# Loading a matrix product's 32-row block tiles in eight pieces on one issuing engine instead of four pieces on two

## The chip, the cores and the metric

One core of a Trainium2 chip. The metric is the device time of one execution in microseconds, median over the runs of a kernel. Each kernel also has one profiled run; its span (first to last instruction) is some 2 us shorter than its time. In names of engines: PE is the matmul engine, DVE, ACT and POOL are the vector, scalar and general engines, SP only issues DMAs; "ACTq" and "SPq" are ACT's and SP's instruction queues. A run is called slow when it is over 1.5% above the fastest of the same kernel.

## The reference

```python
# x: 16 x 512 x 768, weight: 768 x 768, cos and sin: 512 x 64, all float32; 12 heads of 64
y = np.matmul(x, weight).reshape(16, 512, 12, 64)
y1, y2 = y[..., :32], y[..., 32:]
out1 = y1 * cos1 - y2 * sin1
out2 = y2 * cos2 + y1 * sin2
out = np.concatenate([out1, out2], axis=-1).reshape(16, 512, 768)
```

## The kernel before

The input is cut into 64 tiles of 128 rows, worked through as 32 pairs. A tile is loaded (384 KB), cast to fp16 by ACT, turned (rows to columns), multiplied by the weight on PE (12 matmuls), multiplied by cos and sin on DVE, added up on POOL, and stored, one 768 KB store per pair, three pairs later.

There are two ways to turn a tile. A plain tile is turned by six PE transposes and copied back from the accumulator memory by ACT (`xT`). A **block tile**, the second tile of some odd pairs, is loaded so that each 32x32 block lies where DVE can turn it in one instruction, which saves PE 0.34 us. That load is made of four pieces, one per quarter of the partitions.

```python
    def load(n, s):                       # a plain tile, on SP
        ...
        nc.sync.dma_start(out=xss[n, s], in_=...)

    def load_blocks(n):                   # a block tile
        ...
        src = x[b].rearrange("(j a r) (q k) -> r q a j k", r=SB, a=R, q=NQ)
        dst = xss[n, 1].rearrange("p (j k) -> p j k", j=NQ)
        for q in (0, 2, 1, 3):
            eng = nc.sync if q < 2 else nc.scalar
            eng.dma_start(out=dst[ts(q, R)], in_=src[r, q])
    ...
    for n in range(2, NP):
        load_plain(n + AHEAD - 2)
        if n + 1 < NP and by_blocks(n + 1, 1):
            transpose_blocks(n + 1, 1)
        for s in (0, 1):
            for c in CHUNKS:
                mm(n, s, *c)
            upto("turn", 2 * n + s + 3)   # PE transposes, ACT copy to xT
            upto("cast", 2 * n + s + 5)   # ACT
            ...
        if n >= 3:
            store(n - 3, nc.scalar)       # issued by ACT
        load_blocks(n + AHEAD_B)
        if n < NP - ALONE:
            rope_pair(n, 2 * H if n < NP - ALONE - 1 else H)
```

`nc.sync` is SP, `nc.scalar` is ACT, `nc.gpsimd` is POOL. Every engine works through its instructions in order, so an engine that issues DMAs and also computes can be held up by an issue.

## Time and profile before

| | before |
|---|---|
| time, median of 4 runs of the comparison | 164.53 us (164.27 to 165.13) |
| span of the profiled run, granted clock | 162.5 us, 0.988 |
| PE busy | 150.2 us, 92% |
| holes of PE after 17 us, start to start | 2.64 us |
| ACT, DVE, POOL busy | 91.2, 120.8, 110.2 us |
| DMAs per two pairs | 3 plain loads, 4 pieces, 2 stores: 9 |

A hole is the time from the start of one group of matmuls to the start of the next, less what the group takes undisturbed (1.95 us for the 12 matmuls of a tile, 0.34 us for six transposes). Two pairs take PE 4 x 1.95 + 3 x 0.34 = 8.82 us if it never waits. The rows of the page that count the DMA issues will matter (bytes each, then median us from issue to landing):

```profile
out_dram<-ov ACTq DMA_DIRECT2D x31, 768.0 KB, 6.5
xs<-in_x_dram SPq DMA_DIRECT2D x53, 384.0 KB, 6.4
...
xb<-in_x_dram SPq DMA_DIRECT2D x22, 96.0 KB, 6.4
xb<-in_x_dram ACTq DMA_DIRECT2D x22, 96.0 KB, 6.3
```

A piece of 96 KB takes as long from issue to landing as a store eight times its size.

### The profile page before, as it was taken

What the parts mean: (1) busy time and instruction counts of PE and PEld (TensorE: products, weight loads), DVE (VectorE), ACT (ScalarE), POOL (GpSimd) and SP (SyncE); (2) the same over time, 40 slices, a digit from 0 to 9 for tenths busy, and PEclk for the clock granted to TensorE, in tenths of its full rate; (3) what the DMA queues carried; (4) which work ended last, traced back from release to release, by engine and by line L of the source; (5) the groups of instructions that cost most, each with busy time, mean ns of one, the idle gap of its engine ahead of it and who ended that gap; (6) DMA issues with size and microseconds to landing.
All of it is one profiled execution on the core that took longest, in us unless ns stands there. A gap on an engine that the chain in (4) does not pass through costs nothing.

```text
span 162.5 us, 2775 instructions
## 1 busy us (share of the span) xinstructions
PE 150.2 (92%) x1104; PEld 94.4 (58%) x1104; DVE 120.8 (74%) x68; ACT 91.2 (56%) x114; POOL 110.2 (68%) x40
## 2 busy tenths in 40 slices
PE   7799999999998999999999999999989899999910
PEld 2355666666564656666666666666656466666600
DVE  0666976788878587988878787879787756889970
ACT  3431866764665556764765756867293998610000
POOL 0000397777887767778888787877868774699990
PEclk9999999999999999999999999999999999999995
DMA  4999999999999999999999999999997545459766
GB/s 156 358 412 396 403 396 314 384 361 299 381 369 324 399 310 406 316 401 328 405 316 397 350 384 370 371 375 344 320 373 231 196 194 198 194 208 391 283 244 232
DMA packets 24141, 53.17 MB, mean 327 GB/s; under 512 B 2368, under 2 KB 8384, under 8 KB 24128
## 3 DMA queue, kind: packets, MB, share of 16 engines
q1 hardware_dynamic: 12096, 25.89, 47.9%
q10 hardware_dynamic: 12032, 27.10, 43.6%
q8 instruction: 8, 0.13, 0.3%
q14 instruction: 5, 0.04, 0.1%
HBM read 27.82 MB, written 25.17 MB: 326 GB/s over the span
## 4 chain that ended last, share of the span: by engine, by line
PE 51%; DMA 27%; DVE 7%; ACT 6%; issue 2%; ACTq 2%; SPq 1%; POOLq 1%; POOL 1%; DVEq 0%
PE psy L169 43%; DMA xs<-in_x_dram 13%; DMA xb<-in_x_dram 10%; PE pt L126 7%; DVE tq L183 7%; DMA w_raw<-in_weight_dram 4%; ACT xc L76 4%; ACT xT L76 2%; ACTq L243 1%; SPq L83 1%; POOLq L363 1%; POOL ov L194 1%; ACTq L102 0%; ACTq L76 0%; POOLq L194 0%
## 5 line engine op out<-in xcount | busy, mean ns | idle before, releaser
L194 POOL TENSOR_TENSOR ov<-tq 128x1536 f32<-128x1536 f32 (+2 forms) x36 | 110.0, 3067 | 47.9 <-DVE tq L183 47.1
L169 PE MATMUL psy<-w_sb,xT 128*128 128x512 f16 (+1 forms) x744 | 129.7, 326 | 0.8 <-ACT xT L76 0.8
L183 DVE TENSOR_TENSOR tq<-psy,csn 128x3072 f32<-128x3072 f32 (+3 forms) x37 | 103.4, 2807 | 28.7 <-PE psy L169 28.7
L169 PEld LDWEIGHTS <-xT 128*128 128x128 f16 x768 | 72.9, 98 | 45.6 <-ACT xT L76 1.9
L76 ACT COPY xT<-pt 128x768 f16<-128x768 f16 x51 | 40.5, 800 | 36.7 <-PE pt L126 29.2
L76 ACT CAST xc<-xs 128x768 f16<-128x768 f32 x51 | 44.8, 904 | 9.1 <-DMA xs<-in_x_dram 8.1
L126 PE MATMUL pt<-ident,xc 128*128 128x128 f16 x318 | 26.0, 219 | 2.6 <-ACT xc L76 1.6
L126 PEld LDWEIGHTS <-xc 128*128 128x128 f16 x318 | 21.6, 98 | 11.0 <-ACT xc L76 3.6
L76 ACT CAST xc<-xb 128x768 f16<-128x768 f32 x11 | 10.0, 905 | 5.8 <-DMA xb<-in_x_dram 5.8
L247 PE MATMUL cold_ps<-cold 128*128 128x512 f16 x16 | 6.0, 521 | 1.2 <-DVE cold L252 1.2
L133 DVE STREAM_TRANSPOSE xT<-xc 128x384 f32<-128x384 f32 x11 | 6.2, 568 | 0.0
L110 DVE CAST w_sb<-w_raw 128x768 f16<-128x768 f32 x6 | 3.3, 558 | 2.0 <-DMA w_raw<-in_weight_dram 2.0
L78 DVE CAST xc<-xs 128x768 f16<-128x768 f32 x2 | 1.9, 954 | 3.7 <-DMA xs<-in_x_dram 3.7
L169 PE MATMUL psz<-w_sb,xT 128*128 128x512 f16 (+1 forms) x24 | 4.2, 326 | 0.0
L247 PEld LDWEIGHTS <-cold 128*128 128x128 f16 x16 | 1.8, 126 | 3.4 <-issue 2.2
L183 DVE TENSOR_TENSOR tq<-psz,csn 128x1024 f32<-128x1024 f32 (+1 forms) x4 | 3.6, 945 | 0.0
L78 DVE COPY xT<-pt 128x768 f16<-128x768 f16 x2 | 1.1, 556 | 1.3 <-PE pt L126 1.3
L76 ACT ACT_TABLE_LOAD x1 | 1.3, 1283 | 1.1 <-PEq L349 1.1
L252 DVE MEMSET cold<- 128x256 uint32 x1 | 0.3, 272 | 0.9 <-PEq L349 0.9
L148 PE MATMUL psy<-cold 128*128 128x512 f16 x2 | 0.8, 379 | 0.0
L226 DVE TENSOR_TENSOR ov<-psy,tq 128x512 f32<-128x512 f32 x1 | 0.7, 691 | 0.0
L222 DVE TENSOR_TENSOR psy<-psy,csn 128x512 f32<-128x512 f32 x1 | 0.7, 690 | 0.0
(8 smaller groups left out, 1.7 us busy)
## 6 DMA issues: line engine op xcount, KB each, us to landing
out_dram<-ov ACTq DMA_DIRECT2D x31, 768.0 KB, 6.5
xs<-in_x_dram SPq DMA_DIRECT2D x53, 384.0 KB, 6.4
w_raw<-in_weight_dram SPq DMA_DIRECT2D x6, 384.0 KB, 7.6
xb<-in_x_dram SPq DMA_DIRECT2D x22, 96.0 KB, 6.4
xb<-in_x_dram ACTq DMA_DIRECT2D x22, 96.0 KB, 6.3
out_dram<-ov ACTq DMA_DIRECT2D x1, 384.0 KB, 3.4
out_dram<-ov SPq DMA_DIRECT2D x1, 256.0 KB, 2.4
csn<-in_cos_dram SPq DMA_DIRECT2D x1, 128.0 KB, 7.2
```

The source lines that it names most:

```text
L76: eng.copy(out=o, in_=i_)
L78: eng.tensor_copy(out=o, in_=i_)
L83: nc.sync.dma_start(out=xss[n, s], in_=x[b].rearrange("(p r) h -> r p h", r=SB)[r])
L110: nc.vector.tensor_copy(out=w_sb[:, t, e], in_=w_raw[:, t, e])
L126: nc.tensor.transpose(pt[:, t, e, :], xc[:, t, e, :], ident)
L133: nc.vector.transpose(out=xT.bitcast(FP32).rearrange("p t m e -> p (t m e)"), in_=x16.pop((n, s)).bitcast(FP32),)
L169: nc.tensor.matmul(ps, xTT[n, s][:, t, e, :], w_sb[:, t, e, lo:hi], start=((t, e) == CHUNKS[0] and not joined), stop=((t, e) == CHUNKS[-1] ...
L183: nc.vector.tensor_tensor(out=tqs[n][:, :, c0:c1].rearrange("p j (h d) -> p j h d", d=D), in0=ps.rearrange("p (h d) -> p h d", d=D) .unsqu ...
L194: eng.tensor_tensor(out=ovs[n][:, ds(c0, w)].rearrange("p (h t d) -> p h t d", t=2, d=HD), in0=tq[:, 0].rearrange("p (h t d) -> p h t d", ...
L243: eng.dma_start(out=dst, in_=src)
L247: nc.tensor.matmul(cold_ps, cold[:, 0:P], cold, start=True, stop=True)
L363: with _tile.TileContext(nc) as tc:
```

## The change

The intent: free ACT from issuing pieces, keep both halves of the partitions busy by taking lower and upper quarters in turn, issue the pieces earlier, and shorten the end by treating the last eight tiles singly.

```diff
-    AHEAD_B = 4
-    ALONE = 3
+    AHEAD_B = 6
+    ALONE = 4
...
-        return s == 1 and n % 2 == 1 and 6 < n < NP - ALONE
+        return s == 1 and n % 2 == 1 and 8 < n < NP - ALONE
...
-    bpool = ctx.enter_context(tc.tile_pool(name="bpool", bufs=AHEAD_B + 1))
+    bpool = ctx.enter_context(tc.tile_pool(name="bpool", bufs=3))
-    tpool = ctx.enter_context(tc.tile_pool(name="tpool", bufs=9))
+    tpool = ctx.enter_context(tc.tile_pool(name="tpool", bufs=11))
...
-        for q in (0, 2, 1, 3):
-            eng = nc.sync if q < 2 else nc.scalar
-            eng.dma_start(out=dst[ts(q, R)], in_=src[r, q])
+        for q in (0, 1):
+            for j in range(0, NQ, 2):
+                for h in (q, q + 2):
+                    nc.sync.dma_start(
+                        out=dst[ts(h, R), j : j + 2], in_=src[r, h, :, j : j + 2]
+                    )
...
-        k += min(4, max(0, k - 41) // 4)
+        k += min(6, max(0, k - 31) // 4)
...
+                    store(n, nc.scalar, s * H, (s + 1) * H)
-        if n >= 3:
-            store(n - 3, nc.scalar)
         load_blocks(n + AHEAD_B)
         if n < NP - ALONE:
-            rope_pair(n, 2 * H if n < NP - ALONE - 1 else H)
-    store(NP - 3, nc.scalar)
-    store(NP - 2, nc.scalar)
-    store(NP - 1, nc.scalar, 0, H)
+            if n >= 3:
+                store(n - 3, nc.scalar)
+            rope_pair(n, H if n == NP - ALONE - 1 else 2 * H)
+        if n == NP - ALONE - 1:
+            for m in (n - 2, n - 1, n):
+                store(m, nc.scalar)
```

## The prediction

> **What bounds the kernel now.** I read the page's slices first, then the timeline of the matmul engine, then the timeline of ACT where the matmul engine stood still, then the waits of the SP queue, and last the end of the run.
>
> The slices (tenths busy of forty 4.06 us slices, then GB/s):
>
> ```profile
> PE   7799999999998999999999999999989899999910
> DMA  4999999999999999999999999999997545459766
> GB/s 156 358 412 396 403 396 314 384 361 299 381 369 324 399 310 406 316 401 328 405 316 397 350 384 370 371 375 344 320 373 231 196 194 198 194 208 391 283 244 232
> ```
>
> PE is busy nearly throughout, and so is the DMA until the last input lands at about 125 us. Once stores have begun, good slices reach 400 GB/s and every second one sinks to 300-330.
>
> The timeline of PE: one tile is 12 matmuls that start 1.95 us apart from tile to tile, and six PE transposes add 0.34 us. Only four times after the start does the next group come late:
>
> ```profile
> 48.64 2.11 PE L169 MATMUL psy<-w_sb,xT 128*128 128x256 f16 x12
> 51.37 2.12 PE L169 MATMUL psy<-w_sb,xT 128*128 128x512 f16 x12 [0.61 <-ACT xT L76]
> ...
> 60.50 2.12 PE L169 MATMUL psy<-w_sb,xT 128*128 128x512 f16 x12 [0.16 <-ACT xT L76]
> ...
> 120.82 0.51 PE L126 MATMUL pt<-ident,xc 128*128 128x128 f16 x6 [0.46 <-ACT xc L76]
> ...
> 128.61 0.51 PE L126 MATMUL pt<-ident,xc 128*128 128x128 f16 x6 [0.76 <-ACT xc L76]
> ```
>
> The brackets use modelled ends, so I take start to start. 51.37 - (48.64 + 1.95) = 0.78; likewise 60.50 - 60.18 = 0.32, 120.82 - 120.20 = 0.62 and 128.61 - 127.69 = 0.92. Together 2.64 us. So this is a PE-bound kernel with 2.64 us of mid-run holes; the start (until 16.5 us) and the end are something else. No change to loads can win more in the middle than 2.64 us, or 1.6% of 164.56.
>
> The timeline of ACT at those holes says why:
>
> ```profile
> 47.46 3.01 ACTq L102 DMA_DIRECT2D xb<-in_x_dram  x2
> 50.51 0.80 ACT L76 COPY xT<-pt 128x768 f16<-128x768 f16 x1 [2.35 <-DMA xs<-in_x_dram]
> ...
> 117.69 0.89 ACT L76 CAST xc<-xb 128x768 f16<-128x768 f32 x1 [3.01 <-DMA xb<-in_x_dram]
> ...
> 126.17 0.89 ACT L76 CAST xc<-xb 128x768 f16<-128x768 f32 x1 [2.81 <-DMA xb<-in_x_dram]
> ```
>
> At 47-50 us ACT does no arithmetic: its in-order queue is stuck at the issue of a block piece, while a copy to xT waits behind it. At 117 and 126 us it waits for the block tile itself, which was issued late (its ACT pieces at 110.95 and 120.16 us).
>
> Why an issue gets stuck is seen in the trace's records of the DMA issues: in program order, over both queues, they raise eight completion semaphores in turn (99, 101, 103, 104, 105, 107, 108, 109), and each issue first waits for the one eight places earlier. The SP queue's own waits show it, since a load has no other reason to wait for a store:
>
> ```profile
> SPq L83 <- ACT xc L76: 32.3, 17, 6.5
> SPq L83 <- DMA out_dram<-ov: 26.2, 13, 3.8
> ```
>
> So the loads are paced by a window of eight DMAs, not only by the ten xs buffers.
>
> **What the Trainium skill says.** "SBUF — State Buffer", section "Door 1: The DMA port swizzle", says that partitions 0..31 and 0..63 reach the same 8 of 16 ports and measures 189 and 196 GB/s there. The windows view (last column GB/s; plain loads, then twice the two lower quarters alone on SP, then lower on SP with upper on ACT, then upper quarters among stores) agrees:
>
> ```profile
> 25.00:26.00 1.00, 1.00 (x13) 0.73 (x11) 1.00 (x1) 0.51 (x1) 0.90 (x1) 1.00 1.00 386
> 26.50:27.50 1.00, 1.00 (x8) 0.61 (x7) 0.43 (x1) 1.00 (x2) 0.49 (x1) 1.00 1.09 220
> 49.00:50.00 1.00, 1.00 (x8) 0.61 (x7) 1.00 (x2) 0.00 (x0) 0.27 (x1) 1.00 1.16 196
> 32.50:33.50 1.00, 1.00 (x12) 0.73 (x11) 0.72 (x1) 0.46 (x1) 1.00 (x1) 1.00 1.04 345
> 70.25:71.25 1.00, 1.00 (x8) 0.61 (x7) 1.00 (x1) 0.00 (x0) 1.00 (x1) 1.00 1.04 393
> ```
>
> "DMA: Bandwidth & Descriptors", section "Rules for kernel authors", says of two transfers to disjoint halves "Don't bother — they serialize". The 32.5 us line is against that for this traffic: 345 GB/s with both halves in flight, on two rings. Whether pieces in turn on one ring do as well no line here shows. The same page, section "Issuing engines are not separate DMA queues", says that issuing from two engines only saves issue time; here, because of the wait in front, it also decides which engine is stuck.
>
> **The change, part by part.**
>
> 1. *Block pieces leave ACT.* 22 issues go, some 0.49 us each, but ACT is 56% busy, so the issues themselves are worth nothing. What counts is the waits: the holes at 51.37 and 60.50 (0.78 + 0.32) come from them and should close. -1.10 us.
>
> 2. *Pieces earlier* (six pairs ahead, in their place in the order of loads). Before, the last block tile had less than one pair of steps (4.4 us) between issue and the place of its cast, against 6.4 us to landing. After, pair 27 is issued at step 21 and cast at step 23: some 1.5 steps, 6.6 us, and the cast itself stands further ahead of its use. The holes at 120.8 and 128.6 should close. -1.54 us.
>
> 3. *Eight pieces of 48 KB, lower and upper in turn.* Two lower quarters in a row now lose, at 26.25 to 28.5 us, 9 quarter-microseconds at 105 to 203 GB/s under 400: about 0.85 us of transfer per block tile. Balanced halves should lose some 0.3 us. But a pair of steps then has 13 DMAs instead of 9, still with eight semaphores. Worked through the order (one load, store S1, two loads, eight pieces, store S2): piece 4 waits for S2 of the period before, piece 6 for S1 of its own, and all later loads stand behind it on SP. So SP hands out its 1.4 MB in one burst after S1 has landed. A period needs 3.15 MB / 0.4 MB per us = 7.9 us of DMA, plus 0.3, plus a gap of about 1.4 us from the last byte of S1 to the first of the next load (0.3 landing, about 1.2 issue to first packet, as at 157.56 us), part of it filled by loads left over. PE needs 4 x 1.95 + 3 x 0.34 = 8.8 us. This just fits or just fails. A load has about 1.7 steps (7 us) in hand at first and none by step 21, where casts run further ahead. I put 0.6 us of new PE holes for it, as an estimate.
>
> 4. *One block tile fewer* (ten): one more set of PE transposes on the bound engine, +0.34 us. DVE loses a 0.57 us transpose, beside other work.
>
> 5. *Casts up to six tiles further ahead, from index 31 on.* This costs no engine time and gives PE's products slack. But six xc buffers stay: the cast copy of pair 27 is written about step 23.0 and read by DVE's transpose only after the rope of pair 25, at step 26 + 3.9 us, while the cast six places later comes up at step 25 + 2.2 us. ACT stands there some 6 us, and PE, which wants that tile at step 26 + 4.2 us and can have it at + 4.9, loses about 0.7 us. +0.70 us.
>
> 6. *Eight tiles alone, stored singly.* The end is PE, then DVE and POOL behind it:
>
> ```profile
> 141.80 16.55 POOL L194 TENSOR_TENSOR ov<-tq 128x1536 f32<-128x1536 f32 x9 [1.44 <-DVE tq L183]
> ...
> 154.92 0.68 DVE L183 TENSOR_TENSOR tq<-psy,csn 128x512 f32<-128x512 f32 x1
> ```
>
> POOL runs without a gap from 141.80 to 158.35, some 3.5 us after PE's last matmul (154.86). With two more single tiles at 1.75 us each on POOL against 1.95 on PE, counted from the last pair (POOL: 7.9 + 6 x 1.75 + 0.7 = 19.1; PE: 8 x 1.95 = 15.6), it again ends 3.5 us after PE. So no gain there. The 768 KB store issued at 155.94 becomes two of 384 KB, one 1.75 us earlier: the last 1.57 MB before the end become 1.18 MB, but a gap opens in them, so I count -0.30 us.
>
> Sum: -1.10 - 1.54 + 0.60 + 0.34 + 0.70 - 0.30 = -1.30 us; 164.56 - 1.30 = 163.3 us.
>
> **The rivals.**
>
> *The window of eight becomes the bound.* If the burst and gap of part 3 make a period 9.5 us instead of 8.8, ten periods lag 7 us, of which the lookahead swallows most early and little late; 2 to 4 us stay, and the time is 165.5 to 168. For it: the SP queue already waits 26 us for stores. Against: the loads of the kernel before gained some three pairs on the products between 15 and 125 us, so there was room.
>
> *The pieces do not overlap on one ring.* Then all 384 KB of a tile go at some 218 GB/s, losing 0.9 us per tile, as now (0.85). DMA would be as near its limit as before: about 164 to 166. For it: the skill's rule; against: the engines' packets are spread over more than a microsecond in the ring, and 345 GB/s at 32.5 us.
>
> *Everything closes and the end shortens too.* No new holes in parts 3 and 5, and DVE and POOL catch up with PE: -2.64 + 0.34 - 0.9 = -3.2, or 161.4. More than 2% (below 161.27) would need something that I don't see.
>
> **Range and chances.** The middle is between full success (161.4) and the first rival's mild end (166). I give 161.6 to 165.8. Faster by over 2% needs more than all holes: 0.06. Slower by over 2% (above 167.85) needs the first rival at its worst: 0.08. Within 2%: 0.86.
>
> **What would show it right or wrong.** No ACTq issue of xb, and no hole of PE near 50 and 60 us: parts 1 and 2. GB/s of slices between 25 and 110 us no longer sinking to 310-330: part 3, and the second rival wrong. SP waits for out_dram longer than 26 us and new DMA gaps: the first rival. A cast that waits for DVE near pair 26: part 5. POOL's last end 3.5 us after PE's last matmul: part 6. I am wrong if PE shows over 3 us of holes, or if the end after PE's last matmul (7.6 us now) moves by over 1 us.

## The result

| | before | after |
|---|---|---|
| time, median of 4 runs | 164.53 us (164.27 to 165.13) | 179.61 us (177.65 to 181.69) |
| fast runs | all four | 178.53, 177.65 |
| profiled span, granted clock | 162.5 us, 0.988 | 176.8 us, 0.984 |
| ratio of fast runs | | 1.0818 (95%: 1.075 to 1.0886) |

A ratio here and below is the mean time of one kernel's fast runs over the mean of the other kernel's fast runs of the same rounds, so it is not quite the ratio of the medians quoted. The changed kernel is 8% slower, far outside the predicted range. Both profiled runs are fast ones.

The slices of the page after (tenths of PE busy, PE's granted clock, GB/s; each slice is now 4.42 us):

```profile
PE   7899999999959799858969969907999999999940
PEclk9999999999999999999999999996999999999997
GB/s 183 391 407 400 399 400 200 285 330 227 403 86 353 368 346 371 262 261 312 381 202 344 231 380 324 299 203 268 355 411 416 299 164 168 178 359 397 240 251 178
```

From the twelfth slice on PE has holes, and the DMA sinks to 200-260 GB/s in many slices, once to 86, where before it sank to 300-330. So it is not that PE waits for a saturated DMA: both stand at the same time.

PE's timeline (start, length, group, idle before it and its releaser):

```profile
49.08 2.11 PE L172 MATMUL psy<-w_sb,xT 128*128 128x256 f16 x12
53.07 2.12 PE L172 MATMUL psy<-w_sb,xT 128*128 128x512 f16 x12 [1.89 <-ACT xT L76]
...
80.12 2.12 PE L172 MATMUL psy<-w_sb,xT 128*128 128x512 f16 x12 [2.74 <-ACT xT L76]
...
112.90 2.11 PE L172 MATMUL psy<-w_sb,xT 128*128 128x256 f16 x12
120.24 0.80 PE L129 MATMUL pt<-ident,xc 128*128 128x128 f16 x6 [5.23 <-ACT xT L76]
120.84 5.20 PE L172 MATMUL psy<-w_sb,xT 128*128 128x512 f16 x24
```

Start to start, the first hole is 53.07 - (49.08 + 1.95) = 2.04 us. All of them, at 19.03, 42.21, 53.07, 58.95, 72.63, 80.12, 90.60, 103.37 and 120.24, are 0.34 + 0.33 + 2.04 + 1.29 + 0.63 + 2.90 + 1.66 + 1.65 + 5.39 = 16.2 us. After the last one 24 matmuls take 5.20 us where they take 4.06 us elsewhere in this trace: another 1.14 us, in a slice with a granted clock of 0.6. That is 17.4 us, against 2.64 before. With 0.34 us for the additional PE transposes, an earlier start (PE's first transposes after the weight is in, 16.07 instead of 16.50 us) and a tail after PE's last matmul that is 0.60 us shorter (7.03 instead of 7.63), the difference of the spans is explained: 17.4 - 2.64 + 0.34 - 0.43 - 0.60 = 14.1, measured 14.3.

PE waits for ACT's copies to `xT`. ACT's timeline there:

```profile
47.69 0.90 ACT L76 CAST xc<-xb 128x768 f16<-128x768 f32 x1
51.78 0.40 ACTq L246 DMA_DIRECT2D out_dram<-ov  x1
52.22 0.80 ACT L76 COPY xT<-pt 128x768 f16<-128x768 f16 x1 [3.63 <-DMA xb<-in_x_dram]
...
110.78 2.53 ACT L76 CAST xc<-xs 128x768 f16<-128x768 f32 x3
118.97 0.38 ACTq L246 DMA_DIRECT2D out_dram<-ov  x1
119.39 1.50 ACT L76 COPY xT<-pt 128x768 f16<-128x768 f16 x2 [6.09 <-DMA xb<-in_x_dram]
```

A copy has nothing to do with a block tile's DMA. It stands behind a **store** in ACT's queue, and the store stands until a *piece* has landed. Before, ACT was held up by the issue of pieces; now it is held up, longer, by the issue of stores that wait for pieces. The list of waits (us in total, times, longest) has it as a sum; none of these two lines was on the list before:

```profile
ACT xT L76 <- DMA xb<-in_x_dram: 16.6, 4, 6.1
ACT xT L76 <- DMA out_dram<-ov: 11.2, 4, 3.9
```

The SP queue, too, now waits for landings in the pieces' line (L103), though less for stores than before:

```profile
SPq L103 <- DMA xs<-in_x_dram: 24.2, 25, 2.0
SPq L103 <- DMA out_dram<-ov: 6.7, 2, 6.5
```

The chain of waits that sets the end, in order of time, between 103 and 121 us:

```profile
103.49 6.06 DMA out_dram<-ov
...
109.63 0.41 ACTq L246
...
110.53 8.37 DMA xb<-in_x_dram
...
118.97 0.38 ACTq L246
...
119.39 0.81 ACT xT L76
120.24 0.80 PE pt L129 x6
```

A store lands, only then the next store goes out on ACT, behind it comes a piece's issue and landing, only then again a store. Three DMAs one after the other, with their whole latencies.

The records of the DMA issues say why, for instance for one of the eight completion semaphores:

```
semaphore 108 (after)      issued    landed
store, by ACT               40.94     48.04
piece, by SP                48.06     51.39
store, by ACT               51.78
```

10.84 us for one store, one piece and the wake-ups. One more store lies between the two stores, so these are two pairs, which PE would get through in 8.82 us. The rotation that the prediction described (eight semaphores, each DMA waiting for the one eight places earlier) is there, strictly, over SP and ACT together: of the 172 DMAs of the changed kernel that have one eight places before them, none was issued before that one had landed, and so it is in all fourteen traces. It is what the built program does; whether the chip asks for it no run here shows. DVE's block transposes, one per two pairs, come at 50.00 to 147.70 us: nine intervals of 10.86 us, against ten of 9.06 before (40.62 to 131.23).

The rows of DMA issues after:

```profile
out_dram<-ov ACTq DMA_DIRECT2D x28, 768.0 KB, 5.3
xs<-in_x_dram SPq DMA_DIRECT2D x54, 384.0 KB, 6.3
xb<-in_x_dram SPq DMA_DIRECT2D x80, 48.0 KB, 4.1
```

Thirteen DMAs per two pairs instead of nine, and each still takes 4 to 6 us. Two windows in which ACT stands (length; busy time of PE, its weight loads, DVE, ACT, POOL; clock; DMA share; GB/s) show that the DMA engines have little to do at the end of these stands:

```profile
50.00:52.00 2.00, 1.19 (x7) 0.49 (x5) 1.27 (x3) 0.00 (x0) 1.84 (x1) 1.00 0.24 40
118.00:120.00 2.00, 0.00 (x0) 0.00 (x0) 0.47 (x1) 0.61 (x1) 1.45 (x1) 0.93 0.23 47
```

They are not idle throughout: ACT's second stand begins at 113.31 us, and from 113 to 117 us the DMA share was 0.97 at 371 GB/s.

And the end, POOL's timeline: its last six sums begin at 163.29 and end at 172.87, 3.1 us after PE's last matmul (169.73), much as before.

```profile
163.29 9.58 POOL L197 TENSOR_TENSOR ov<-tq 128x768 f32<-128x768 f32 x6
```

### The profile page after: what moved, and what is told of

Same layout as the page of the kernel before. It is cut to its first block, busy times and chain, and to the rows that moved or that the text cites. A ratio compares the mean times of both kernels' runs of the same rounds, so it can differ in the third digit from the quotient of the medians.

```text
span 176.8 us, 2861 instructions
## 1 busy us (share of the span) xinstructions
PE 153.2 (87%) x1110; PEld 96.1 (54%) x1110; DVE 120.6 (68%) x70; ACT 90.8 (51%) x115; POOL 110.1 (62%) x41
## 4 chain that ended last, share of the span: by engine, by line
PE 44%; DMA 41%; ACT 4%; DVE 3%; issue 2%; POOL 1%; ACTq 1%; SPq 1%; POOLq 0%; DVEq 0%
PE psy L172 32%; DMA xs<-in_x_dram 17%; DMA out_dram<-ov 12%; DMA xb<-in_x_dram 12%; PE pt L129 6%; PE cold_ps L250 3%; DVE tq L186 3%; PE psz L172 2%; ACT xT L76 2%; ACT xc L76 2%; POOL ov L197 1%; ACTq L246 1%; SPq L103 1%; POOLq L367 0%; SPq L83 0%
## 5 line engine op out<-in xcount | busy, mean ns | idle before, releaser
L76 ACT COPY xT<-pt 128x768 f16<-128x768 f16 x52 | 41.3, 800 | 55.8 <-PE pt L129 22.9
L76 ACT CAST xc<-xs 128x768 f16<-128x768 f32 x52 | 45.8, 900 | 7.3 <-DMA xs<-in_x_dram 7.2
L129 PE MATMUL pt<-ident,xc 128*128 128x128 f16 x324 | 27.2, 223 | 7.2 <-ACT xT L76 5.7
L129 PEld LDWEIGHTS <-xc 128*128 128x128 f16 x324 | 22.8, 100 | 15.8 <-issue 6.6
L76 ACT CAST xc<-xb 128x768 f16<-128x768 f32 x10 | 9.0, 904 | 0.0
L250 PE MATMUL cold_ps<-cold 128*128 128x512 f16 x16 | 6.7, 569 | 1.2 <-DVE cold L255 1.2
L172 PE MATMUL psz<-w_sb,xT 128*128 128x512 f16 (+1 forms) x36 | 6.3, 326 | 0.0
L186 DVE TENSOR_TENSOR tq<-psz,csn 128x512 f32<-128x512 f32 (+1 forms) x5 | 4.3, 896 | 0.1
L229 DVE TENSOR_TENSOR ov<-psz,tq 128x512 f32<-128x512 f32 x1 | 0.7, 691 | 0.0
```

The costliest lines, as they stand in the source:

```text
L76: eng.copy(out=o, in_=i_)
L129: nc.tensor.transpose(pt[:, t, e, :], xc[:, t, e, :], ident)
L172: nc.tensor.matmul(ps, xTT[n, s][:, t, e, :], w_sb[:, t, e, lo:hi], start=((t, e) == CHUNKS[0] and not joined), stop=((t, e) == CHUNKS[-1] ...
L186: nc.vector.tensor_tensor(out=tqs[n][:, :, c0:c1].rearrange("p j (h d) -> p j h d", d=D), in0=ps.rearrange("p (h d) -> p h d", d=D) .unsqu ...
L250: nc.tensor.matmul(cold_ps, cold[:, 0:P], cold, start=True, stop=True)
```

## The experiments

**Theory W (window):** the loss is the *number* of DMAs that go through the rotation of eight, 13 per two pairs instead of 9, whatever they carry. **Rivals:** T, the way the pieces travel (48 KB, halves in turn on one ring) costs transfer time; C, the rest of the change (casts further ahead, singles at the end, fewer block tiles) costs it; D, each small DMA costs something in itself, wherever it is issued. All results below were correct.

### e1, e2, e3: one part undone, one part alone

e1 is the changed kernel with four pieces, still all on SP:

```diff
-        for q in (0, 1):
-            for j in range(0, NQ, 2):
-                for h in (q, q + 2):
-                    nc.sync.dma_start(
-                        out=dst[ts(h, R), j : j + 2], in_=src[r, h, :, j : j + 2]
-                    )
+        for q in (0, 2, 1, 3):
+            nc.sync.dma_start(out=dst[ts(q, R)], in_=src[r, q])
```

> The changed kernel, but each block tile in four pieces of 96 KB (lower, upper, lower, upper), all on SP. A period of two pairs then has 9 DMAs instead of 13, as before the change. Theory W (eight completion semaphores: the number of DMAs per period is the cost, and ACT's stores get stuck behind pieces): most of the 15 us goes away, 163 to 168 us. Theory T (all pieces on one ring go through too few ports at a time; the transfer itself is the cost): still 175 us or more. Theory C (the rest of the change is the cost): still 175 or more.

e2 is the kernel before with nothing but the eight pieces on SP (the reverse of that hunk, applied to before).

> The kernel before with only the eight pieces on SP put in; lead, buffers and end as before. W and T: slower by most of the 15 us, 172 to 182 us. C: as before, 164 to 166 us.

e3 is the changed kernel with the loading of before (four pieces, two on SP, two on ACT).

> The changed kernel with the old four pieces (two on SP, two on ACT), everything else of the change kept. W: 162 to 167 us, since there are again 9 DMAs per period. T: 162 to 166. C: 175 or more.

| | time, us | ratio to before (95%) | holes of PE after 17 us |
|---|---|---|---|
| before, 7 runs | 164.63 | | 2.6 |
| e1 four pieces | 161.21 (160.87 to 161.37) | 0.9798 (0.9738 to 0.9858) | 0 |
| e2 pieces alone | 175.75 (175.33 to 179.08) | 1.067 (1.0604 to 1.0736) | 14.4 |
| e3 rest alone | 164.60 (163.89 to 165.19) | 0.9999 (0.9937 to 1.0061) | 2.8 |

By the means of the fast runs the eight pieces alone cost 11.0 of the 13.5 us, the rest alone nothing: C falls as the main cause. The other 2.5 us come only with both together, and no run tells why. And with four pieces in their place, the changed kernel is *faster* than before, by more than I had expected (163 to 168 us). That it is faster is clear of the noise; whether by over 2% is not, here and for e6, e9, e10 and e12 below. PE's slices and the GB/s of e1:

```profile
PE   7899999999999999999999999999999999999920
...
GB/s 147 373 406 402 398 401 365 318 389 231 410 346 378 360 221 411 380 391 411 402 408 379 351 402 397 397 380 411 412 346 160 200 198 201 178 394 378 239 198 198
```

PE has no hole between 17 us and the end. The two early dips in GB/s (231, 221) cost it nothing.

### e4, e5: more DMAs without bytes, in and out of the rotation

e4 is the kernel before with four additional loads of 4 KB per block tile, issued by SP; nothing reads what they load.

```diff
+        for k in range(4):
+            extra = epool.tile([16, D], FP32, tag="extra", name="extra")
+            nc.sync.dma_start(out=extra, in_=cos[ts(k, 16)])
```

> The kernel before with four extra loads of 4 KB on SP beside each block tile: 13 DMAs per period, almost no extra bytes, the block pieces unchanged. The tiny ones hold their semaphore for less time than a piece (some 2 to 3 us). W: slower by 4 to 12 us, 168 to 177. T and C: as before, 164 to 166.

e5 issues the same loads from POOL. The records of its issues show that POOL's DMAs raise eight other semaphores (111 to 118).

```diff
-            nc.sync.dma_start(out=extra, in_=cos[ts(k, 16)])
+            nc.gpsimd.dma_start(out=extra, in_=cos[ts(k, 16)])
```

> As the run with four extra 4 KB loads per block tile, but these are issued by POOL, whose DMAs raise eight other semaphores in the built program; the rotation of SP and ACT is back at 9 DMAs per period. Theory W (the rotation of eight is the cost): 164 to 168 us, some loss allowed for POOL's own issuing. Theory D (every small DMA costs, whoever issues it, in the DMA engines): still 175 or more.

Measured: e4 186.07 us (184.23 to 187.33), ratio 1.1213 (1.1122 to 1.1304); e5 166.17 us (165.80 to 166.65), ratio 1.012 (1.0053 to 1.0186). The rows of the additional loads, e4 first (its profiled run was a slow one; I use only the latency), then e5:

```profile
extra<-in_cos_dram SPq DMA_DIRECT2D x44, 4.0 KB, 4.0
```

```profile
extra<-in_cos_dram POOLq DMA_DIRECT2D x44, 4.0 KB, 5.3
```

The additional loads carry 0.18 MB of 53 MB, and on SP they cost 12%. So it is not the bytes (T), and as the same loads cost only 1.2% where they take other semaphores, it is not each small DMA in itself (D). POOL's DMAs also go through a queue of their own (q0 on the page), so neither e5 nor e8 below tells the semaphores from the queue; for the semaphores speaks that no issue in any trace breaks the rotation. A load of 4 KB holds its place in the rotation for 4.0 us, not the 2 to 3 that I expected, and much as a piece of 48 KB (4.1). e4 went beyond what I had expected, a miss. A part of it is clock: its two fast runs had a granted clock of 0.964 and 0.949, those of the changed kernel 0.984 and 0.974. Why else it costs more than eight real pieces is open.

### e6 and e9: four pieces on SP alone, and their order

e6 is the kernel before with its four pieces all on SP, in the order lower, upper, lower, upper.

```diff
-            eng = nc.sync if q < 2 else nc.scalar
-            eng.dma_start(out=dst[ts(q, R)], in_=src[r, q])
+            nc.sync.dma_start(out=dst[ts(q, R)], in_=src[r, q])
```

> The kernel before with only its four pieces moved: all four on SP, lower and upper in turn; nothing else of the change. If the gain of the four-piece version of the change (161.2) comes from the pieces alone, 161 to 162.5; if lead and end are needed too, 163 to 165.

e9 is e6 in the order lower, lower, upper, upper.

```diff
-        for q in (0, 2, 1, 3):
+        for q in (0, 1, 2, 3):
```

> As the kernel before with only its four pieces moved to SP (161.4), but in the order lower, lower, upper, upper. If lower and upper in turn is what frees the transfer: DMA slices sink again and some holes of PE return, 162.5 to 165. If it is enough that ACT issues no pieces: 161.2 to 162.

Measured: e6 161.38 us (161.29 to 161.71), ratio 0.9833 (0.976 to 0.9907); e9 161.66 us (161.23 to 161.81), ratio 0.978 (0.9734 to 0.9826). Neither has a hole of PE after 19 us. So the gain of e1 is there without the rest of the change: it is that ACT no longer issues pieces. The order of the halves, lower and upper in turn or not, shows no effect.

### e8: the eight pieces kept, the stores taken out of the rotation

```diff
-                store(n - 3, nc.scalar)
+                store(n - 3, nc.gpsimd)
...
-                store(m, nc.scalar)
+                store(m, nc.gpsimd)
```

> The changed kernel with its eight pieces kept, but the stores of pairs 0 to 27 issued by POOL: they leave the rotation of eight, and ACT no longer stands at a store's issue. Theory W with ACT stuck at its stores as the path: 161 to 168. If eight small pieces are slow in themselves, or SP's pacing alone does it: 174 or more. POOL's issuing may cost something of its own.

Measured: 163.10 us (162.94 to 163.25), ratio 0.9931 (0.9869 to 0.9993). PE's slices and two of the rows of DMA issues:

```profile
PE   7899999999999999999999999999999999999700
```

```profile
out_dram<-ov POOLq DMA_DIRECT2D x28, 768.0 KB, 6.6
...
xb<-in_x_dram SPq DMA_DIRECT2D x80, 48.0 KB, 5.8
```

The same eighty pieces of 48 KB, slower to land (5.8 instead of 4.1 us), and PE has no hole: T falls for good. SP issues the same eleven DMAs per two pairs as in the changed kernel, so its own time for issuing is not the loss either. e8 is 2 us slower than e1, all of it behind PE: the last matmul starts at 151.88 us (e1: 151.83). POOL, which now issues the stores, is busy 129 us instead of 110.

### e11, e12: the eight pieces and the stores in the rotation, but ACT freed

e8 takes the stores out of the rotation *and* frees ACT of them. To tell the two apart, e11 keeps the rotation with its thirteen DMAs but has SP issue the stores, so that ACT cannot stand at one.

```diff
-                store(n - 3, nc.scalar)
+                store(n - 3, nc.sync)
...
-                store(m, nc.scalar)
+                store(m, nc.sync)
```

> The changed kernel with its eight pieces, but the stores of pairs 0 to 27 issued by SP instead of ACT, in their places. The rotation of eight semaphores and its 13 DMAs per two pairs stay as they are; only ACT no longer stands at them. Theory A (the loss is ACT standing at store issues, with the copies for PE behind it): PE's holes go, 161 to 164 us. Theory B (the serial order of store, piece, store starves the loads whoever issues them): 172 us or more, PE's holes stay and follow casts that wait for loads. Between the two, 165 to 171 us, both have a share. Note that SP may also stand for POOL's results, which the run with four pieces and the same stores controls.

e12 is the control: the same edit on e1, with four pieces.

> The control: four pieces on SP, and the stores of pairs 0 to 27 on SP too. If issuing stores from SP is harmless in itself, 160.5 to 163 us, as with four pieces and stores on ACT (161.2). If SP stands for POOL's results with the loads behind it, over 164 us, and then the run with eight pieces is to be read against this one.

Measured: e11 177.17 us (176.04 to 178.56), ratio 1.0779 (1.07 to 1.0858); e12 161.45 us (160.89 to 161.62), ratio 0.9813 (0.975 to 0.9876). I had leaned to "ACT standing is the loss", since every large hole of the changed kernel has a stuck store in front of it. **As a forecast for e11 that falls.** With ACT free, the loss is as large; it only comes later and by another way. e11's PE timeline:

```profile
88.50 2.11 PE L172 MATMUL psy<-w_sb,xT 128*128 128x256 f16 x12
91.71 0.51 PE L129 MATMUL pt<-ident,xc 128*128 128x128 f16 x6 [1.10 <-ACT xc L76]
...
101.65 0.51 PE L129 MATMUL pt<-ident,xc 128*128 128x128 f16 x6 [2.14 <-ACT xc L76]
101.99 5.74 PE L172 MATMUL psy<-w_sb,xT 128*128 128x256 f16 x24
```

Until 91 us PE has no hole. Then its holes follow casts, and those wait for plain loads that come too late. The waits of casts for `xs` in the whole run, of e11 and then of the changed kernel (us in total, times, longest):

```profile
ACT xc L76 <- DMA xs<-in_x_dram: 36.7, 16, 4.9
```

```profile
ACT xc L76 <- DMA xs<-in_x_dram: 7.2, 2, 4.4
```

Before the change it was 8.1 us. So in the changed kernel loads were not late, and its holes are those of copies stuck behind stores; e11 does not show that ACT's standing was harmless there. It shows that stores in the rotation of thirteen cost as much when SP stands at them, with the loads behind. SP's timeline shows how late SP is, still before the first hole:

```profile
79.87 5.47 SPq L103 DMA_DIRECT2D xb<-in_x_dram  x8
85.43 0.46 SPq L246 DMA_DIRECT2D out_dram<-ov  x1
85.93 0.47 SPq L83 DMA_DIRECT2D xs<-in_x_dram  x1
86.50 0.89 SPq L246 DMA_DIRECT2D out_dram<-ov  x1
87.43 2.52 SPq L83 DMA_DIRECT2D xs<-in_x_dram  x2
90.05 0.90 SPq L103 DMA_DIRECT2D xb<-in_x_dram  x1
```

From the first piece of one block tile to that of the next it is 10.2 us here, and 10.83 us on average over the nine intervals from 22.85 to 120.35; PE needs 8.82. In e12 it is 8.80 us (23.12 to 102.32). Nine times (10.83 - 8.82) is 18.1 us, and e11's span is 176.8 - 159.6 = 17.2 us longer than e12's. A part of those 18 us is hidden at first by the tiles loaded ahead, which is why the first hole comes only at 91 us; the late holes in their turn delay POOL's sums, the stores and the loads behind them, and cost clock. e11's SP has more to issue than the changed kernel's, so its period is not quite the same case; the control shows that issuing the stores from SP costs nothing by itself.

### e7, e10: is there more to gain?

e7 takes both tiles of an odd pair as block tiles, with one set of four pieces of 192 KB for both, on e1; it also has eight instead of ten `xs` buffers, which was not tested alone.

```diff
-        return s == 1 and n % 2 == 1 and 8 < n < NP - ALONE
+        return n % 2 == 1 and 8 < n < NP - ALONE
...
+        src = x[b : b + 2].rearrange("b (j a r) (q k) -> r q a b j k", r=SB, a=R, q=NQ)
+        dst = xb.rearrange("p b (j k) -> p b j k", j=NQ)
...
+        if n + 2 < NP and by_blocks(n + 2, 0):
+            transpose_blocks(n + 2, 0)
```

> Four-piece version of the change, and in the odd pairs both tiles come as blocks, in the same four DMAs of 192 KB: 8 DMAs per period instead of 9 and ten more tiles without PE transposes. The four-piece version has no hole of PE after 17 us, so 10 x 0.34 us should come off: 157.8 us by theory W, 157 to 160 allowed. If DVE's ten more transposes or the bigger lower-half bursts get in the way: 161 or more.

Measured: 160.74 us in one run and 164.70 to 166.53 us in three slow ones, so there is no ratio. In its profile (a slow run) casts wait 14.7 us for `xb`. A miss: even the best run is only 0.5 us below e1, where 3.4 were forecast. What makes it swing is open, and so is whether the three slow runs are its usual state.

e10 is e1 with two more block tiles, in pairs 5 and 7, loaded early.

```diff
-        return s == 1 and n % 2 == 1 and 8 < n < NP - ALONE
+        return s == 1 and n % 2 == 1 and 4 < n < NP - ALONE
```

> Four-piece version of the change with two more block tiles, in pairs 5 and 7. That version has no hole of PE after 17 us, so its time should fall by 2 x 0.34 us of PE transposes: 160.3 to 160.9 us. If the early loads, with no stores yet and all buffers filling, get in the way: 161.2 or more.

Measured over six runs: 161.80 us (160.73 to 162.25), ratio 0.9786 (0.9747 to 0.9824), the same as e1 within the intervals. Two sets of transposes less are 0.68 us of PE; one hole of 0.69 us at 103.99 us in the profiled run (160.73, the fastest) takes it back. A miss too. So four pieces on SP are the version to keep, as in e1 (161.21 us) or, with the smallest edit, e6 (161.38), which the runs do not tell apart; both beat the kernels before and after.

## Why the prediction was wrong

**Part 3 is the step that failed.** It had the rotation of eight semaphores with 13 DMAs per two pairs right. What failed is its term, 0.60 us of new holes from "This just fits or just fails", and the path by which it let the rotation act, over late loads on SP alone. It measured 14.8 us more of holes and lost clock in the changed kernel (17.4 - 2.64), 14.4 us of holes in all with nothing but the pieces changed (e2), and PE waited for copies stuck behind ACT's stores. Three things were wrong in it.

1. *The period was worked out from bytes.* I took 7.9 us for the bytes plus one gap of 1.4 us, and did not count places. If N DMAs per period share eight places, a place can be held for 8/N of a period on average. As an estimate from the page of before: with N = 9 and L = 6.4 us from issue to landing the period must be at least 9/8 x 6.4 = 7.2 us, which fits into 8.82; with N = 13 it is 13/8 x 6.4 = 10.4 us, which doesn't. These numbers stood on the page, and would have warned me. But the count is a warning and does not size the loss. With the changed kernel's own landings, (2 x 5.3 + 3 x 6.3 + 8 x 4.1)/13 = 4.8 us, it gives 7.8 us, which would fit, and with those of e8, which has 11 in the rotation and no hole, 11/8 x (3 x 6.6 + 8 x 5.8)/11 = 8.3 us. SP started a block load every 9.82 us in the changed kernel (22.12 to 110.53), every 10.83 in e11 and every 9.11 in e8 (22.24 to 104.22). What the count leaves out is the strict order: a free place stays empty while an issue before it is stuck. SP stood until 48.06 us at the one piece whose place a store held (semaphore 108 above); the next four places, raised from 48.43 to 51.24 us, had then been free for 6.2 to 7.6 us.
2. *Only SP's side was looked at.* I worked out which pieces wait for which stores, and not that ACT's stores take places in the same rotation and wait for pieces just issued. So ACT stood, with PE's copies behind it: up to 6.1 us, where before a copy had come up to 2.4 us late behind a stuck issue. e11 shows that the loss is as large when SP stands at the stores instead.
3. *The lookahead was trusted.* "Of which the lookahead swallows most": for the loads of the changed kernel that came true, but tiles loaded ahead do not help a copy that is stuck behind a store. Where the loads themselves are late, e11 shows how far the lookahead reaches, to 91 us of 177. Ten tiles of buffers hide a lag once and not a period that is too long.

The first rival, "The window of eight becomes the bound", was thus right in kind. Its period of 9.5 us is near SP's 9.82; its time of 165.5 to 168 us is far below 179.6, since it counted late loads less the lookahead, and not ACT at its stores.

**Part 1 was right about the cause and hidden in the result.** No ACT issue of a piece is left. But the holes near 50 and 60 us stayed (53.07: 2.04 us, 58.95: 1.29 us), for the stores took the pieces' place as what ACT stands at. With four pieces, e1 and e6, all the mid-run holes are gone; what I had as "Everything closes and the end shortens too", 161.4 us, is what e1 measured, 161.21. Of e1's 3.4 us of span, 2.64 are holes, less 0.34 of transposes; the start (16.23 against 16.50) and tail (7.00 against 7.63 us after the last matmul) give 0.27 and 0.63, 3.2 us together. That the number agrees is partly luck: it was meant for eight pieces.

**Part 2** can't be told from part 1: e6 closes the late holes too, without issuing the pieces earlier. **Part 4** is right by the count of instructions (six more PE matmuls of 0.056 us). **Part 5**, the ACT wait near pair 26 (+0.70 us), did not come: e1 has the same six `xc` buffers and the same casts ahead, and no hole. **Part 6** was right in kind: the tail got 0.60 us shorter (0.30 predicted), and POOL still ends 3.1 us after PE (3.5 predicted).

The rival "The pieces do not overlap on one ring" is ruled out as the cause by e8 and e9. Its 218 GB/s stands on no line shown; at the 220 GB/s of the line at 26.50 us a tile of 393 KB takes 0.8 us longer than at 400, not 0.9. In part 3, 0.3 and 1.2 us make 1.5 and not 1.4; neither slip matters. Of the things that were to show me wrong, "over 3 us of holes" did, and "SP waits for out_dram longer than 26 us" did not: they fell to 7.9 us, as the wait moved to ACT and to SP's waits for loads.

**What stays open:** why 4 KB loads cost more than real pieces (e4), what makes e7 swing, and the 2.5 us between e2 and the changed kernel. I have not varied the number of semaphores, so their part in it rests on e4, e5 and e8 and on the records of the issues, and how N sets the loss is not shown.

## What to carry to other kernels

Before cutting a DMA into smaller ones, count the DMAs per period that share completion semaphores, and compare N/8 times the landing time on the page with the period that the compute needs (here 10.4 against 8.82 us). Take it as a warning and not as the size of the loss. Pieces as small as 4 KB held a place for 4 us here, so cutting them smaller frees little; issue them from an engine that has nothing else to do. And when an in-order engine is seen stuck at an issue, freeing that engine moves the wait to the next one. Ask what stands behind it there: with 9 DMAs in the rotation nothing was lost (e6, e12), with 13 as much as in the changed kernel (e11).

## What the Trainium skill lacked or had wrong

- "DMA: Bandwidth & Descriptors", section "Issuing engines are not separate DMA queues": it says that issuing from several engines only saves issue time. It lacks that the wait in front of an issue can be for an unrelated DMA of the other engine, and what that costs: 3.63 and 6.09 us of ACT here. The choice of engine was worth 1.7% with four pieces (e6, ratio 0.9833).
- The same page, section "Rules for kernel authors": to coalesce small transfers points the right way, but by their overhead. It lacks the count of DMAs in flight: 4 KB loads on SP cost 12% (e4), and on POOL, with other semaphores and another queue, 1.2% (e5). Of two transfers to disjoint halves it says that they serialise; this case can't tell how far they do, but agrees in the consequence, as the halves in turn on one ring (161.38 us, ratio 0.9833) or one after the other (161.66 us, ratio 0.978) made no difference. None of the pages that I looked up states the rotation of eight semaphores over SP and ACT, with its strict order.
- "TensorE: Matmul & The Clock Gate", section "Part 1: The HAM clock gate", says that PE's clock halves after an idle window of about 3.4 us. The hole of 5.39 us agrees: 1.14 us more were lost behind it. But in e11 a hole of 2.31 us (at 101.65 us) was enough. The window just behind it, by windows (clock, DMA share and GB/s last), has a granted clock of 0.57, while the changed kernel, after its hole of 2.90 us at 80.12 us, has a clock of 1.00 in the window from 80 to 83 us:

```profile
99.00:102.00 3.00, 0.86 (x11) 0.46 (x10) 1.68 (x1) 1.28 (x2) 1.24 (x1) 1.00 1.03 397
102.00:106.00 4.00, 4.00 (x18) 1.95 (x16) 0.12 (x1) 3.33 (x5) 2.20 (x1) 0.57 0.85 290
```
